# Weight halves in tiles of their own, and middle units of wide products run by row block, in a two-layer decoder trunk

## The chip, the cores and the metric

The kernel runs on one core of a Trainium2 chip. The metric is the device time of one execution in microseconds (us); the time of a version is the median of its runs. In the profile PE is the matrix engine (TensorE) and PEld its loading of the 128x128 operand, DVE is VectorE, ACT is ScalarE, POOL is GpSimd, and SP is the engine that issues the loads of the weights.

## The reference

Input are 256 tokens of width 2048, 256 memory tokens, and the f32 weights of two layers. A layer is a token mixer, a cross attention into the memory, and a squared-ReLU MLP, each one as x + norm(f(norm(x))).

```
for i in range(2):
    x = x + rms_norm(mixer_i(rms_norm(x)))          # i = 0: mLSTM, i = 1: gated DeltaNet
    x = x + rms_norm(cross_attention(rms_norm(x), mem))
    x = x + rms_norm(relu(rms_norm(x) @ w_up) ** 2 @ w_down)     # 2048 -> 8192 -> 2048
```

The mixer of layer 1, where most of what follows takes place, projects to q, k (16 heads of 128), v (32 heads of 128), z and the gates, runs q, k and v through a causal convolution of four taps and a silu, and solves a unit triangular system in chunks of 64 tokens:

```
q, k = l2_norm(silu(conv(q))), l2_norm(silu(conv(k)));  v = silu(conv(v))
g    = -exp(a_log) * softplus(a + dt_bias);  gam = cumsum(g)
A    = (k*beta) @ k.T * exp(strict_lower(gam_i - gam_j))
U, W = solve(I + A, v*beta), solve(I + A, k*beta*exp(gam))
```

## The kernel before

Some 500 MB of f32 weights are streamed from memory once, in **units** of 2048 columns per partition. `Weights` (L33 to L112) holds the list of all units in the order of use. A unit of a wide or a token product covers 4 row blocks of 128 by 512 columns, a **tall** unit (the products gq, gk and gv, and a few small ones) 16 row blocks by 128 columns. A unit is loaded in two halves of 512 KB by SP's queue (L74) into tiles `raw`, of which there are four. Each half is then split for the matrix engine: ACT copies it to the rounded type fp32r as `hi` (L88 CAST), and DVE takes `lo = raw - hi` (L89). Two tiles `hi` and two tiles `lo` of 8 KB per partition, each for a whole unit, turn around. `take` hands the oldest unit to a product and first begins those up to two ahead (L98).

Each product is the sum of hi*hi, hi*lo and lo*hi. The wide products (`prod_feat`, L286: k_m, q, k, o, up, and wide parts of the others) take one hi matmul of 512 columns (both parts of the activations) and one lo matmul of 256 (L314, L315), for 4 column blocks f times 4 row blocks j of a unit. The first unit of a product goes over all f for each j, every other one over all j for each f (L306 to L308). `prod_tall` (L325) takes a unit's 16 row blocks in order with three matmuls of 256 columns each (L333, L334 on hi, L335 on lo), so the second half's tiles come after 24 of its 48 matmuls. `prod_tok` (L356) has tokens as the stationary operand, three matmuls of 512 columns (L378, L379 on lo, L380); v, xq, xo, down, gz and g_out are of this kind.

The order of the instructions on each engine is not written out: a scheduler in the framework lists them from the program's order, the tiles' lifetimes and estimated times, and each engine then runs its list in order. When a tile is freed earlier or later on paper, instructions of all engines can change places.

In layer 1's mixer the q and k products run in four rounds (`prod_q`, `prod_k`, L949 and on). Beside them stand, per round, the convolutions of the blocks just made (`conv`: `pad` and three `cv` on DVE, one `cv` L868 and a silu L871 on ACT), `norms` (squares `l2sq` L962 on ACT, column sums `l` L966 on PE, an rsqrt L266 on ACT) and twice `pairs` (L969): `decays` multiplies masks into `gl` on POOL, sums them on PE (`gep`, L937) and takes 12 exps on ACT (`gdm`, L941); k times q and k times k on PE (`g`, L983, L984) are scaled on DVE and ACT (`gm`, L986 to L990) and multiplied with `gdm` on DVE (`at`, L994). Silu, exp and the rsqrt need tables that ACT loads when it goes from one to another (ACT_TABLE_LOAD). The gates run once before that: a softplus on DVE and ACT (`sp_e`, `sp_u`), then `g` (L913) and a matmul `suf` (L919). After the rounds come the v blocks (`prod_v`, with transposes `vp` L884) beside the solve, whose intermediate tensors go out and in by POOL's queue (`t_d`, `tn_d`, `ab`).

Of the kernel before, what the change touches and what calls it, by code (L numbers as in the profile page):

```python
# [8 lines left out]
F32R = mybir.dt.float32r  # L9
# [5 lines left out]
P = 128  # L15
# [19 lines left out]
class Weights:  # L35
# [18 lines left out]
    def begin(self, place=None):  # L54
# [8 lines left out]
        un = UN * UK // kb  # L63
        if place:
            hi, lo = zip(*(place(j) for j in range(kb)))
        else:
            ht = self.hi.tile([P, kb, un], F32R, tag="hi", name=f"hi{i}")
            lt = self.lo.tile([P, kb, un], F32R, tag="lo", name=f"lo{i}")
            hi, lo = ([t[:, j, :] for j in range(kb)] for t in (ht, lt))
        halves = []  # L70
        hb = kb // 2
        for k0 in range(0, kb, hb):
            raw = self.raw.tile([P, hb, un], F32, tag="raw", name=f"raw{i}_{k0}")
            nc.sync.dma_start(raw[:, :, :n], src[k0 * P : (k0 + hb) * P, :].rearrange("(kb p) n -> p kb n", p=P))  # L74

            def split(k0=k0, raw=raw):
                if kb == KB and n < P:
                    h_, l_ = ht[:, k0 : k0 + hb, 0:n], ht[:, k0 : k0 + hb, n : 2 * n]
                    a = nc.scalar.copy(h_, raw[:, :, :n])
                    return a, nc.vector.tensor_tensor(l_, raw[:, :, :n], h_, ALU.subtract)  # L80
                if place:
                    for j in range(hb):
                        h_ = hi[k0 + j][:, :n]
                        a = nc.scalar.copy(h_, raw[:, j, :n])
                        v = nc.vector.tensor_tensor(lo[k0 + j][:, :n], raw[:, j, :n], h_, ALU.subtract)
                    return a, v
                h_, l_ = ht[:, k0 : k0 + hb, :n], lt[:, k0 : k0 + hb, :n]
                a = nc.scalar.copy(h_, raw[:, :, :n])  # L88
                return a, nc.vector.tensor_tensor(l_, raw[:, :, :n], h_, ALU.subtract)  # L89
# [21 lines left out]
def trunk(ctx: ExitStack, tc, x, mem, norm_g, mem_norm_g, w_mem_kv, w_xq, w_xo, w_up, w_down,  # L111
# [5 lines left out]
    const = ctx.enter_context(tc.tile_pool(name="const", bufs=1))  # L117
    ws = Weights(tc, ctx, ahead=2, bufs=(4, 2, 2))
    acts = ctx.enter_context(tc.tile_pool(name="acts", bufs=1))
# [172 lines left out]
    def prod_feat(key, srcs, n_fb, evac, wide=True, before=None, fresh=False):  # L292
# [3 lines left out]
        for c0 in range(0, n_fb, 4):  # L296
            nf = min(4, n_fb - c0)
            accs, k = None, 0
            while k < nk:
# [6 lines left out]
                order = [(f, j) for f in range(nf) for j in range(kb)]  # L306
                if c0 == 0 and k == 0:
                    order = [(f, j) for j in range(kb) for f in range(nf)]  # L308
# [929 lines left out]
```

## Time and profile before

| what | value |
|---|---|
| time, median of 3 runs | 2954.86 us (2952.91 to 2958.61) |
| the profiled execution, its time / span | 2962.7 us / 2960.6 us |
| mean granted TensorE clock of it | 0.993 |
| PE busy | 2911.2 us (98%), 16595 matmuls |
| DVE / ACT / POOL busy | 1746.1 (59%) / 1443.7 (49%) / 137.1 us (5%) |
| bytes moved | 553.15 MB, mean 187 GB/s |

The page gives busy time by engine and the chain of work that ended last. Where one engine is busy nearly everywhere, the busy time by stretches of 100 us shows where it is not; the list of its waits by what released them, and the timeline of a stretch (one row per instruction, with the idle time before it and its releaser in brackets) then show why. Matmuls overlap, so the time from one start to the next, and not a row's duration, is what a matmul costs in a dense stretch.

### The profile page before, as it was taken

The numbers are of one execution on the slowest core, as the hardware profiler recorded it, in microseconds if no ns is written. First come the engines' busy times: TensorE is split into PE (matmuls) and PEld (weight loads), VectorE is DVE, ScalarE is ACT, GpSimd is POOL, SyncE is SP. The second block draws the span as 40 slices with busy tenths as digits, with TensorE's granted clock in tenths as the row PEclk, the third lists the DMA queues.
The fourth block names the chain that finished last, engine by engine and source line by source line (L and its number), as shares of the span: only waits on it lengthen the run. The fifth ranks groups of instructions, "written<-read, shape, count | busy, mean of one in ns | idle before, by whom it ended". The sixth has DMA issues, their size and how long they took to land.

```text
span 2960.6 us, 42191 instructions
## 1 busy us (share of the span) xinstructions
PE 2911.2 (98%) x16595; PEld 2504.0 (85%) x16595; DVE 1746.1 (59%) x2544; ACT 1443.7 (49%) x2213; POOL 137.1 (5%) x256
## 2 busy tenths in 40 slices
PE   8999999999999999999999999999999999999998
PEld 7888888988888888898889977877888888888887
DVE  5555657654645555677778844444567546455565
ACT  6444546544434444566664544444456444344343
POOL 0000000000000000013321011000000000000000
PEclk9999999999999999999999999999999999999999
DMA  7545565556655556556778755655445565555565
GB/s 232 178 157 158 192 199 167 168 186 194 189 189 187 193 186 196 180 150 167 204 204 226 240 200 182 212 182 172 162 149 185 186 197 185 191 191 189 188 190 170
DMA packets 373960, 553.15 MB, mean 187 GB/s; under 512 B 22769, under 2 KB 155378, under 8 KB 371458
## 3 DMA queue, kind: packets, MB, share of 16 engines
q1 hardware_dynamic: 363456, 507.12, 55.1%
q0 software_dynamic: 8736, 42.02, 4.1%
q8 instruction: 130, 2.13, 0.3%
q10 hardware_dynamic: 1570, 1.33, 0.1%
q14 instruction: 68, 0.56, 0.1%
HBM read 527.29 MB, written 23.10 MB: 186 GB/s over the span
## 4 chain that ended last, share of the span: by engine, by line
PE 92%; DMA 3%; DVE 3%; ACT 1%; issue 1%; DVEq 0%; ACTq 0%; SPq 0%
PE up L314 15%; PE up L315 8%; PE down L378 8%; PE down L380 8%; PE down L379 8%; DMA raw<-in_gdn_w_in 2%; PE gz L378 2%; PE gz L380 2%; PE gz L379 2%; PE g_out L378 2%; PE g_out L380 2%; PE g_out L379 2%; PE o L314 2%; PE gv L335 2%; PE gv L333 2%; PE gv L334 2%
## 5 line engine op out<-in xcount | busy, mean ns | idle before, releaser
L89 DVE TENSOR_TENSOR lo<-raw,hi 128x1024 fp32r<-128x1024 f32 x938 | 1121.4, 1224 | 901.3 <-ACT hi L88 900.4
L88 ACT CAST hi<-raw 128x1024 fp32r<-128x1024 f32 x938 | 947.6, 1046 | 972.2 <-PE down L380 310.8
L314 PE MATMUL up<-h,hi 128*128 128x512 f32 x1920 | 678.7, 399 | 0.0
L315 PE MATMUL up<-h,lo 128*128 128x256 f32 x1920 | 539.2, 281 | 0.0
L314 PEld LDWEIGHTS up<-h,hi 128*128 128x128 f32 x1920 | 360.8, 188 | 89.8
L379 PE MATMUL down<-lo,u 128*128 128x512 f32 x1024 | 398.4, 389 | 0.0
L378 PE MATMUL down<-hi,u 128*128 128x512 f32 x1024 | 398.4, 389 | 0.0
L380 PE MATMUL down<-hi,u 128*128 128x512 f32 x1024 | 398.3, 389 | 0.0
L315 PEld LDWEIGHTS up<-h,lo 128*128 128x128 f32 x1920 | 362.7, 189 | 0.2
L380 PEld LDWEIGHTS down<-hi,u 128*128 128x128 f32 x1024 | 192.2, 188 | 40.0
L378 PEld LDWEIGHTS down<-hi,u 128*128 128x128 f32 x1024 | 192.2, 188 | 40.0
L379 PEld LDWEIGHTS down<-lo,u 128*128 128x128 f32 x1024 | 192.2, 188 | 39.6
L333 PE MATMUL gv<-h,hi 128*128 128x256 f32 x512 | 148.6, 290 | 1.7 <-ACT hi L88 1.7
L335 PE MATMUL gv<-h,lo 128*128 128x256 f32 x512 | 147.9, 289 | 0.8 <-DVE lo L89 0.8
L334 PE MATMUL gv<-h,hi 128*128 128x256 f32 x512 | 147.6, 288 | 0.0
L378 PE MATMUL gz<-hi,h 128*128 128x512 f32 x256 | 103.7, 405 | 0.0
L380 PE MATMUL gz<-hi,h 128*128 128x512 f32 x256 | 103.0, 402 | 0.0
L333 PEld LDWEIGHTS gv<-h,hi 128*128 128x128 f32 x512 | 100.7, 197 | 2.7 <-ACT hi L88 2.3
L379 PE MATMUL gz<-lo,h 128*128 128x512 f32 x256 | 102.5, 400 | 0.0
L335 PEld LDWEIGHTS gv<-h,lo 128*128 128x128 f32 x512 | 100.6, 197 | 1.5 <-DVE lo L89 1.5
L334 PEld LDWEIGHTS gv<-h,hi 128*128 128x128 f32 x512 | 100.8, 197 | 0.3 <-issue 0.2
L378 PE MATMUL g_out<-hi,u 128*128 128x512 f32 x256 | 100.9, 394 | 0.0
(412 smaller groups left out, 4728.4 us busy)
## 6 DMA issues: line engine op xcount, KB each, us to landing
raw<-in_w_up SPq DMA_DIRECT2D x256, 512.0 KB, 3.9
raw<-in_w_down SPq DMA_DIRECT2D x256, 512.0 KB, 4.2
raw<-in_gdn_w_in SPq DMA_DIRECT2D x192, 512.0 KB, 4.9
raw<-in_mlstm_w_in SPq DMA_DIRECT2D x96, 512.0 KB, 4.0
raw<-in_gdn_w_out SPq DMA_DIRECT2D x64, 512.0 KB, 4.2
raw<-in_mlstm_w_out SPq DMA_DIRECT2D x32, 512.0 KB, 4.4
at_d<-at POOLq DMA_DIRECT2D x8, 1536.0 KB, 7.6
ab<-at_d POOLq DMA_DIRECT2D x8, 1536.0 KB, 8.6
```

Of the source, the lines that this page charges most:

```text
L88: a = nc.scalar.copy(h_, raw[:, :, :n])
L89: return a, nc.vector.tensor_tensor(l_, raw[:, :, :n], h_, ALU.subtract)
L314: PE.matmul(a[:fw], wh, srcs[kk][:, :], start=(kk == 0), stop=False, skip_group_check=True)
L315: PE.matmul(a[:fw, T:], wl, srcs[kk][:, 0:T], start=False, stop=(kk == nk - 1), skip_group_check=True)
L333: PE.matmul(a[:, 0:T], hi[k], srcs[k][:, 0:T], start=(k == 0), stop=False)
L334: PE.matmul(a[:, 0:T], hi[k], srcs[k][:, T:], start=False, stop=False)
L335: m = PE.matmul(a[:, 0:T], lo[k], srcs[k][:, 0:T], start=False, stop=(k == nk - 1))
L378: PE.matmul(accs[t], sh, hi[j], start=(kk == 0), stop=False)
L379: PE.matmul(accs[t], sh, lo[j], start=False, stop=False)
L380: PE.matmul(accs[t], sl, hi[j], start=False, stop=(kk == nk - 1))
```

## The change

The tiles `hi` and `lo` are taken per half unit: four of 4 KB each in place of two of 8 KB, so that the space is the same and each half is freed when its own last matmul is done. The cast L88 and the subtraction L89 (L93 and L94 in the new file, where lines behind them are 5 higher) write the same elements as before. In `prod_feat` the units that are neither first nor last of a product now also go over all f for each j, so that their first half is done after 16 of their 32 matmuls.

```diff
@@ -61,21 +61,26 @@
         k, n = src.shape
         kb, i = k // P, self.done
         un = UN * UK // kb
-        if place:
-            hi, lo = zip(*(place(j) for j in range(kb)))
-        else:
-            ht = self.hi.tile([P, kb, un], F32R, tag="hi", name=f"hi{i}")
-            lt = self.lo.tile([P, kb, un], F32R, tag="lo", name=f"lo{i}")
-            hi, lo = ([t[:, j, :] for j in range(kb)] for t in (ht, lt))
+        hi, lo = [], []
         halves = []
         hb = kb // 2
         for k0 in range(0, kb, hb):
             raw = self.raw.tile([P, hb, un], F32, tag="raw", name=f"raw{i}_{k0}")
             nc.sync.dma_start(raw[:, :, :n], src[k0 * P : (k0 + hb) * P, :].rearrange("(kb p) n -> p kb n", p=P))
-
-            def split(k0=k0, raw=raw):
+            if place:
+                ht = lt = None
+                ph, pl = zip(*(place(j) for j in range(k0, k0 + hb)))
+                hi += ph
+                lo += pl
+            else:
+                ht = self.hi.tile([P, hb, un], F32R, tag="hi", name=f"hi{i}_{k0}")
+                lt = self.lo.tile([P, hb, un], F32R, tag="lo", name=f"lo{i}_{k0}")
+                hi += [ht[:, j, :] for j in range(hb)]
+                lo += [lt[:, j, :] for j in range(hb)]
+
+            def split(k0=k0, raw=raw, ht=ht, lt=lt):
                 if kb == KB and n < P:
-                    h_, l_ = ht[:, k0 : k0 + hb, 0:n], ht[:, k0 : k0 + hb, n : 2 * n]
+                    h_, l_ = ht[:, :, 0:n], ht[:, :, n : 2 * n]
                     a = nc.scalar.copy(h_, raw[:, :, :n])
                     return a, nc.vector.tensor_tensor(l_, raw[:, :, :n], h_, ALU.subtract)
                 if place:
@@ -84,7 +89,7 @@
                         a = nc.scalar.copy(h_, raw[:, j, :n])
                         v = nc.vector.tensor_tensor(lo[k0 + j][:, :n], raw[:, j, :n], h_, ALU.subtract)
                     return a, v
-                h_, l_ = ht[:, k0 : k0 + hb, :n], lt[:, k0 : k0 + hb, :n]
+                h_, l_ = ht[:, :, :n], lt[:, :, :n]
                 a = nc.scalar.copy(h_, raw[:, :, :n])
                 return a, nc.vector.tensor_tensor(l_, raw[:, :, :n], h_, ALU.subtract)
 
@@ -115,7 +120,7 @@
     V, S, G, PE = nc.vector, nc.scalar, nc.gpsimd, nc.tensor
 
     const = ctx.enter_context(tc.tile_pool(name="const", bufs=1))
-    ws = Weights(tc, ctx, ahead=2, bufs=(4, 2, 2))
+    ws = Weights(tc, ctx, ahead=2, bufs=(4, 4, 4))
     acts = ctx.enter_context(tc.tile_pool(name="acts", bufs=1))
     tmp = ctx.enter_context(tc.tile_pool(name="tmp", bufs=2))
     small = ctx.enter_context(tc.tile_pool(name="small", bufs=2))
@@ -304,7 +309,7 @@
                 if accs is None:
                     accs = [acc(f"{key}{c0 + f}") for f in range(nf)]
                 order = [(f, j) for f in range(nf) for j in range(kb)]
-                if c0 == 0 and k == 0:
+                if (c0 == 0 and k == 0) or 0 < k < nk - kb:
                     order = [(f, j) for j in range(kb) for f in range(nf)]
                 w_ = wide and not (fresh and c0 == 0)
                 for f, j in order:
```

PE, DVE, POOL and SP execute the same instructions as before; ACT has 16 ACT_TABLE_LOAD more (67 in place of 51). Where they stand differs. The first place is PE in the second round of q and k, at the second pair group. `gk1` to `gk3` are column blocks of the k product with the units 224 to 226, `h8` its row block 8, the first of a unit's second half. Before:

```order
L983 MATMUL g0_11389<-gqk1_10431 128x512
L984 MATMUL g1_11390<-gqk1_10431 128x256
L937 MATMUL gep_11683<-gl00_11684,tri_gt_r_10420 128x512
L333 MATMUL gk1_11487<-h8_10283,hi224_11409 128x256
L334 MATMUL gk1_11487<-h8_10283,hi224_11409 128x256
L937 MATMUL gep_11683<-gl01_11686,tri_gt_r_10420 128x512
L333 MATMUL gk2_11555<-h0_10275,hi225_11477 128x256
L334 MATMUL gk2_11555<-h0_10275,hi225_11477 128x256
L937 MATMUL gep_11694<-gl10_11695,tri_gt_r_10420 128x512
```

and now, from the same matmul of `g` on:

```order
L988 MATMUL g0_11831<-gqk1_10851 128x512
L989 MATMUL g1_11832<-gqk1_10851 128x256
L339 MATMUL gk1_11933<-h8_10701,hi224_8_11857 128x256
L340 MATMUL gk1_11933<-h8_10701,lo224_8_11858 128x256
L338 MATMUL gk1_11933<-h9_10702,hi224_8_11857 128x256
```

followed by the rest of unit 224 without a break, to the first matmuls of units 225 and 226 and two of `gep`:

```order
L340 MATMUL gk1_11933<-h15_10708,lo224_8_11858 128x256
L338 MATMUL gk2_12003<-h0_10693,hi225_0_11923 128x256
L339 MATMUL gk2_12003<-h0_10693,hi225_0_11923 128x256
L338 MATMUL gk3_12073<-h0_10693,hi226_0_11993 128x256
L339 MATMUL gk3_12073<-h0_10693,hi226_0_11993 128x256
L942 MATMUL gep_12133<-gl00_12134,tri_gt_r_10840 128x512
L942 MATMUL gep_12133<-gl01_12136,tri_gt_r_10840 128x512
```

Unit 224's second half stood behind the matmuls of `gep` and was cut in two by them; now it follows at once, `gep` stands a unit later, and its last two pairs later still.

The second place is ACT at the same point, from the scaling of `gm` on. Before:

```order
L990 ACTIVATE gm_11376<-g0_11377,rk_11339 128x2x128
L88 CAST hi224_11409<-raw224_8_11413 128x1024
L868 ACTIVATE cv_11471<-pad_11468,cols_98 128x256
L88 CAST hi225_11477<-raw225_0_11479 128x1024
L88 CAST hi225_11477<-raw225_8_11481 128x1024
L990 ACTIVATE gm_11388<-g0_11389,rk_11339 128x2x128
L941 ACTIVATE gdm_11681<-gep_11683,lnb_11025 128x128 x2
L941 ACTIVATE gdm_11682<-gep_11683,lnb_11025 128x128 x2
L941 ACTIVATE gdm_11681<-gep_11694,lnb_11025 128x128 x2
L941 ACTIVATE gdm_11682<-gep_11694,lnb_11025 128x128 x2
L941 ACTIVATE gdm_11681<-gep_11705,sufb_11036 128x128 x2
L941 ACTIVATE gdm_11682<-gep_11705,sufb_11036 128x128 x2
```

and now:

```order
L995 ACTIVATE gm_11818<-g0_11819,rk_11781 128x2x128
L873 ACTIVATE cv_11915<-pad_11912,cols_98 128x256
L93 CAST hi225_0_11923<-raw225_0_11921 128x1024
L93 CAST hi225_8_11927<-raw225_8_11925 128x1024
L93 CAST hi226_0_11993<-raw226_0_11991 128x1024
L995 ACTIVATE gm_11830<-g0_11831,rk_11781 128x2x128
L93 CAST hi226_8_11997<-raw226_8_11995 128x1024
L946 ACTIVATE gdm_12131<-gep_12133,lnb_11459 128x128 x2
L946 ACTIVATE gdm_12132<-gep_12133,lnb_11459 128x128 x2
L93 CAST hi227_0_12063<-raw227_0_12061 128x1024
L876 ACT_TABLE_LOAD
L876 ACTIVATE gqk4_11472<-cv_11915 128x256
```

The cast of unit 224's second half has gone ahead of the first pair group's exps (out of these rows), four casts stand ahead of the second group's, and its 12 exps are no longer in one piece: four, then a silu with a table load before it, then the others in pieces between silus, each with a table load. This holds in all four rounds.

The third place is PE at the `suf` matmul of the gates, in the q product ahead of the rounds, before:

```order
L333 MATMUL gq2_11188<-h8_10283,hi221_11110 128x256
L334 MATMUL gq2_11188<-h8_10283,hi221_11110 128x256
L919 MATMUL suf_11034<-g_11027,tri_gt_95 128x32
L335 MATMUL gq2_11188<-h8_10283,lo221_11111 128x256
L333 MATMUL gq2_11188<-h9_10284,hi221_11110 128x256
```

and now:

```order
L339 MATMUL gq2_11628<-h2_10695,hi221_0_11548 128x256
L340 MATMUL gq2_11628<-h2_10695,lo221_0_11549 128x256
L924 MATMUL suf_11468<-g_11461,tri_gt_95 128x32
L338 MATMUL gq2_11628<-h3_10696,hi221_0_11548 128x256
L339 MATMUL gq2_11628<-h3_10696,hi221_0_11548 128x256
```

It stood at row block 8 of its unit, and now stands behind row block 2, 17 matmuls earlier.

## Rows read from the trace of the kernel before

**Rows 1.** The page: busy time by engine.

```profile
PE 2911.2 (98%) x16595; PEld 2504.0 (85%) x16595; DVE 1746.1 (59%) x2544; ACT 1443.7 (49%) x2213; POOL 137.1 (5%) x256
```

**Rows 2.** Windows of 100 us: busy us (instructions) by engine, PEclk, DMA share, GB/s.

```profile
700.00:800.00 100.00, 100.00 (x555) 86.28 (x555) 59.21 (x84) 46.89 (x69) 0.00 (x0) 1.00 0.59 186
1300.00:1400.00 100.00, 95.21 (x698) 88.91 (x698) 71.59 (x123) 64.53 (x111) 33.42 (x48) 0.97 0.58 158
```

**Rows 3.** What PE waited for: us in total, times, longest us.

```profile
PE gk L335 <- DVE lo L89: 5.3, 6, 1.2
PE l L966 <- ACT l2sq L962: 2.5, 3, 1.1
PE gv L333 <- ACT hi L88: 1.7, 2, 1.2
PE gk L333 <- ACT hi L88: 1.6, 3, 0.5
...
PE xo L379 <- DVE lo L89: 1.1, 2, 0.5
...
PE gv L335 <- DVE lo L89: 0.8, 1, 0.8
PE suf L919 <- DVE g L913: 0.6, 1, 0.6
```

**Rows 4.** Windows at the second pair groups of the three rounds and of the fourth.

```profile
1332.00:1342.00 10.00, 7.44 (x42) 5.29 (x41) 10.00 (x13) 8.75 (x20) 7.53 (x8) 1.00 0.28 93
1398.00:1408.00 10.00, 7.47 (x44) 5.42 (x43) 10.00 (x12) 8.85 (x19) 8.03 (x9) 1.00 0.34 112
...
1524.00:1532.00 8.00, 7.23 (x44) 5.66 (x43) 8.00 (x13) 7.72 (x19) 2.44 (x5) 1.00 0.42 139
```

**Rows 5.** Timeline of PE there, first round: start us, us, line, op [idle before <-releaser].

```profile
1333.77 0.39 PE L333 MATMUL gk<-h,hi 128*128 128x256 f32 x1 [0.54 <-ACT hi L88]
...
1336.38 0.39 PE L335 MATMUL gk<-h,lo 128*128 128x256 f32 x1 [0.56 <-DVE lo L89]
1336.60 0.28 PE L333 MATMUL gk<-h,hi 128*128 128x256 f32 x1
1336.72 0.28 PE L334 MATMUL gk<-h,hi 128*128 128x256 f32 x1
...
1341.34 0.39 PE L335 MATMUL gk<-h,lo 128*128 128x256 f32 x1 [1.21 <-DVE lo L89]
```

**Rows 6.** Timeline of ACT, same stretch, from the first group's exps on.

```profile
1325.79 1.91 ACT L941 ACTIVATE gdm<-gep,lnb 128x128 f32<-128x128 f32 x7
...
1331.34 1.03 ACT L88 CAST hi<-raw 128x1024 fp32r<-128x1024 f32 x1
...
1334.93 2.16 ACT L941 ACTIVATE gdm<-gep,lnb 128x128 f32<-128x128 f32 x8
1336.93 1.19 ACT L941 ACTIVATE gdm<-gep,sufb 128x128 f32<-128x128 f32 x4
1339.19 1.05 ACT L88 CAST hi<-raw 128x1024 fp32r<-128x1024 f32 x1 [1.06 <-PE gk L334]
```

**Rows 7.** Timeline of DVE, same stretch.

```profile
1331.52 1.83 DVE L994 TENSOR_TENSOR at<-gm,gdm 128x768 f32<-128x768 f32 x2
...
1336.25 3.50 DVE L994 TENSOR_TENSOR at<-gm,gdm 128x768 f32<-128x768 f32 x2
```

**Rows 8.** Groups by line and form, PE: line, op, names, count | busy us, mean ns | idle.

```profile
L314 PE MATMUL up<-h,hi 128*128 128x512 f32 x1920 | 678.7, 399 | 0.0
...
L314 PE MATMUL o<-h,hi 128*128 128x512 f32 x256 | 89.0, 392 | 0.0
```

**Rows 9.** Groups of ACT, 1236 to 1560 us: table loads for silu.

```profile
L871 ACT ACT_TABLE_LOAD x10 | 12.8, 1283 | 0.2
```

**Rows 10.** Timeline of ACT at the solve's end, the cast that PE waits for.

```profile
1688.06 1.04 ACT L88 CAST hi<-raw 128x1024 fp32r<-128x1024 f32 x1 [6.45 <-PE gv L335]
```

**Rows 11.** Window behind the solve's end, at the half clock.

```profile
1691.00:1694.40 3.40, 3.40 (x18) 3.40 (x17) 2.28 (x5) 1.43 (x3) 0.00 (x0) 0.50 0.74 187
```

## The prediction, made before the change was run

> **What bounds the kernel now.** I read the page's first part first: PE is busy for 2911.2 of 2960.6 us [rows 1], so all that any edit can win without shortening matmuls is about 49 us. The windows of 100 us say where those lie. In the MLP's stretches PE is busy for 100.00 of 100.00 us, where layer 1's q and k are made for 95.21 [rows 2]. Then I read the list of PE's waits, and kept those that end with a weight half, since the change is about these: lo for gk 5.3 us in 6 waits, hi for gk 1.6 us in 3, hi and lo for gv 1.7 and 0.8, lo for xo 1.1 [rows 3]. That is 10.5 us in all, and no wide product is on the list. The edit's evident aim, weights a half unit earlier, can so win in few places.
>
> The main place is the second pair group of each round. In the window of 10 us there PE is busy for 7.44 us in the first round and 7.47 in the second (the third is like it), and in the fourth, beside gv, for 7.23 of 8.00 [rows 4]: 2.56 + 2.53 + 2.53 + 0.77 = 8.4 us idle. The timeline shows three stops for a weight half, of 0.54, 0.56 and 1.21 us [rows 5], and the timeline of ACT why: after the exps of the first group, begun at 1325.79, the cast of the next half begins at 1331.34; then come 2.16 + 1.19 us of exps, and the next cast begins at 1339.19 [rows 6]. On DVE two `at` products take 3.50 us in that place against 1.83 for two a little earlier [rows 7], because DVE shares this stretch with POOL's masks (an inference: POOL is busy for 7.53 of these 10 us [rows 4]). So PE waits for casts that stand behind exps in ACT's order, and for lo behind `at` in DVE's.
>
> **The change part by part.** *Wide products, units run by row block first.* Costed at nothing. No wait for a weight stands there (`up` and o have an idle of 0.0 [rows 8]), and ACT and DVE with their casts and subtractions are busy for only 47 and 59 us of 100 [rows 2], so the earlier release is hidden by a PE that is never late. The order itself could cost or win through PE's pace: the hi matmul of `up` takes 399 ns on average, that of o 392 [rows 8], with the same shapes, and both have units of either order, since the first unit of a product is by row block already. If all 1920 of `up` went over to o's pace, 1920 x 7 ns = 13.4 us would be won; if the 512 of q, k and o went over to that of `up`, 512 x 7 ns = 3.6 us lost. I take 0, since in the trace the pace goes with the product and not with the order; the ends stay for the range.
>
> The Trainium skill (TensorE: Matmul & The Clock Gate, "Why this matters for your kernels") speaks against row blocks first: it wants all K tiles of one output tile in a row before going on. By its reasons the order matters where PE waits between them; by this trace PE does not wait there at all, so the sum by the rule is the same 0 as long as the units stay dense.
>
> *Rounds of q and k.* The order shows the cast of a unit's second half ahead of the first group's exps, four casts ahead of the second group's, and unit 224 run without a break. So the waits for hi of 0.54 us and for lo of 0.56 and 1.21 us [rows 5] lose their cause. Each stop also costs a slower restart: the first matmul after it takes 0.39 us against 0.28 in a dense stretch [rows 5], 0.1 us, four stops to a round. A round now loses 2.54 + 0.4 = 2.9 us. What stays: the lo of units 225 and later still stands among `gm` and `at` on DVE, which the change leaves slow (3.50 us [rows 7]); I leave 0.9 us, between nothing and the 0.56 + 1.21 = 1.8 us that the two waits for lo keep if they only go to a later unit. That gives 2.0 us a round, 6.0 for three, with bounds of 8.7 won (all gone) and, were a round's wait to grow by one more pair of `at`, 3 x (3.5 - 2.0) = 4.5 lost. For the fourth, beside gv, 0.77 + 0.1: I take 0.9, bounds 0 and 1.1.
>
> *The 16 table loads.* Each takes 1283 ns [rows 9], so 20.5 us more on ACT, 5.1 in each of four rounds of about 64 us. ACT is busy for 64.53 of 100 us there [rows 2], so of 64 us about 23 are free, and 5.1 fit. They are costed at nothing: what hides them is this idle time, and a cast that may come late by the slack between its unit and PE, which is up to a unit, 48 matmuls x 0.12 us = 5.8 us (from one start to the next they take 0.12 us in a dense stretch [rows 5]). If that cover is gone the price is up to 5.1 us a round, the second rival.
>
> *The gates.* `suf` waits for `g` on DVE now (0.6 us [rows 3]) and moves 17 matmuls earlier, 17 x 0.12 = 2.0 us, while what makes `g` (softplus on DVE and ACT) is not shortened. If `g` comes as now, PE stands for 2.0 us longer; if the matmul that feeds the chain and two casts ahead of its table load (1.05 us each [rows 6]) also delay it, 4.1. At best the chain moves up with it and the cost is 0. I take 2.0, as the nearest row, bounds 0 and 4.1. Queued behind `suf` on PE are the other matmuls of gq, nothing that another engine is short of.
>
> *End of the solve.* PE waits there once for hi of gv, 1.2 us of the 1.7, and 0.8 for lo [rows 3], and behind it 3.40 us run at the granted clock 0.50 [rows 11], that is at 1.2 GHz, after a PE that stood still; half of these 3.4 us, 1.7, is the loss. The cast waited 6.45 us for a matmul's release of a tile [rows 10], and a half tile is released up to 24 matmuls, 2.9 us, earlier. So the 2.0 go and half of the clock's loss: -2.9, bounds 0 (the raw half is not there sooner, since POOL's transfers fill the DMA engines) and -3.7.
>
> *xo.* 1.1 us [rows 3] in two layers. Its casts can start when half a unit is free. I take -1.1, bounds 0 and -1.1 (an end with more in it has no row).
>
> *The rest.* SP's queue gives out the same loads with the same four `raw` tiles. The waits of `l` for `l2sq`, 2.5 us [rows 3], stand behind squares that do not move; 0. Clock windows elsewhere may come and go, 1.7 us each as at the solve: ±3 for the range.
>
> Sum: 0 - 6.0 - 0.9 + 0 + 2.0 - 2.9 - 1.1 = -8.9 us. The profiled execution took 2962.7 us and would take 2953.8. It is 7.8 us above the median of the runs, 2954.86; the terms are stalls that every run should have, so I take the sum off the median: **2946.0 us**.
>
> **The rivals.** *The wait only moves.* PE, no longer stopped at the second pair group, comes 2.9 us sooner to `l`, which waits for `l2sq` already (0.8 us on average [rows 3]), or to weights that the loads do not bring sooner. Then the rounds' 6.9 us come back, and what is left is 2.0 - 2.9 - 1.1 = -2.0: 2952.9 us, no difference that can be measured (0.2%, 5.9 us, is about what a measurement of this kernel tells from none). For it: l2sq is made on ACT behind the same exps and table loads. Against it: of the three waits for `l`, the longest is 1.1 us, while a round's idle time at the pair group is 2.5. That the halves are not cast sooner, because `raw` and not `hi` is what is missing, ends in the same place: without the solve's term and xo's, and with half of the rounds', -3.4 + 2.0 = -1.4, 2953.4 us.
>
> *The split exps reach PE.* ACT runs its list in order. In place of one block of exps it now goes exp, silu, exp, silu, with a table load each; a silu waits for `cv` on DVE, and casts stand behind it. If the casts between them come a load and a silu's wait too late, PE stops once for each. Price: 5.1 us a round in four, 20.5, against the -8.9 of the sum: 2954.9 - 8.9 + 20.5 = 2966.5 us, slower. It decides from the point at which the loads and waits in a unit's 5.8 us, with 2 casts (2.1 us), a `cv` and a silu (0.9), exceed what is left, 2.8 us: two table loads (2.6) and one exp make that full. For it speaks that some units get two loads; against it that other units have the whole 2.8 us free and casts can run ahead by a unit.
>
> The Trainium skill (ScalarE: Activation LUTs, "Table sets: the hidden batching unit") gives the rule that this breaks: all activations of one set together, then those of the next. It puts a switch at 2.66 us including a drain, by which 16 would cost 42.6 us of ACT; the trace shows 1283 ns a load and the next activation directly behind it, so the price above goes by the trace.
>
> *PE's pace changes.* `up` goes over to o's pace: -8.9 - 13.4 = -22.3, 2932.6 us. For it: the two paces exist with the same shapes. Against it: units by row block first occur at the start of `up` and go no faster.
>
> **How the numbers follow.** The forecast has 0.50, and with it go 2937 to 2953 (all bounds for the better; rounds halved and the gates at their worse end). The wait that moves and the missing `raw` together 0.28, the exps that reach PE 0.16, the pace 0.06. Faster by over 0.2%: 0.50 + 0.06 = 0.56; within: 0.28; slower: 0.16. The range reaches to the pace's case at 2932 and on the other side to 2962, three quarters of the exps' price; outside is the worst of the exps' case and a pace that goes with all terms for the better.
>
> **What would show it right or wrong.** In the list of PE's waits gk for lo and hi falls from 6.9 us to under 3, gv's 2.5 to under 1, xo's 1.1 to about 0, and `suf` grows from 0.6 to about 2.6. In the windows at the pair groups PE is busy for over 9 us of 10. ACT's table loads in the rounds rise by 16, with ACT near 70 of 100 us. `up` keeps 399 ns. Wrong would be: waits for l or for a DMA grown by what gk's lost, waits for hi behind a table load, or wide matmuls of another mean length.

## The result and the profile after

| | median | runs | lowest to highest |
|---|---|---|---|
| before | 2953.56 us | 20 | 2949.28 to 2958.61 |
| changed | 2960.39 us | 20 | 2956.22 to 2964.23 |

The ratio is 1.0023 with a 95% interval of 1.0016 to 1.0030: the change costs about 7 us. Forecast were 2946.0 us and, with 0.56, a gain; the time lies inside the range of 2932 to 2962, on the side that had 0.16.

The page hardly shows it. Busy time by engine of the changed kernel, in answer to [rows 1]:

```profile
PE 2911.4 (98%) x16595; PEld 2501.9 (85%) x16595; DVE 1777.1 (60%) x2544; ACT 1496.4 (51%) x2229; POOL 140.7 (5%) x256
```

PE has the same work; ACT has 52.7 us more, of which 20.5 are the 16 table loads and some 30 come from casts that overlap each other less (a cast takes 1047 ns on average, 1046 before). The two profiled executions took 2962.7 and 2961.98 us, so their traces alone would have shown no loss; the one of before was longer than all of its other runs (2949 to 2959), the one of after is within its own. What they lost the time to differs, and the list of PE's waits shows it. In answer to [rows 3]:

```profile
PE g L989 <- ACT gdm L946: 12.7, 4, 3.4
PE ltp L215 <- DVE xk L495: 10.1, 9, 1.8
...
PE gk L340 <- DVE lo L94: 3.6, 3, 1.3
PE l L971 <- ACT l2sq L967: 2.6, 3, 1.1
...
PE gv L340 <- DVE lo L94: 0.2, 1, 0.2
PE suf L924 <- DVE g L918: 0.2, 1, 0.2
```

Most of the waits that the prediction counted did go: gk for hi is no longer there (1.6), gk for lo is 3.6 for 5.3, gv's two are 0.2 for 2.5, xo's have gone, `vp`'s 2.7 and `gep`'s 1.0 too (both from the list of before), and `suf` is 0.2 for 0.6. In their place stands one that was not on the list before: the matmul `g` waits for the exps `gdm`, four times, 12.7 us in all, the longest 3.4. The whole list comes to 40.1 us before and 39.4 now: what the half tiles won, `g` took back.

The windows in answer to [rows 2] show the MLP's stretch dense as before (PE busy for all of 700 to 800 us) and the rounds as bad as before, with ACT at 68.68 for 64.53:

```profile
1300.00:1400.00 100.00, 95.07 (x705) 89.49 (x704) 70.91 (x118) 68.68 (x116) 32.95 (x46) 0.97 0.56 152
```

In answer to [rows 8] the mean of `up`'s hi matmul is the same, and that of o has gone from 392 to 399 ns:

```profile
L319 PE MATMUL up<-h,hi 128*128 128x512 f32 x1920 | 678.7, 399 | 0.0
...
L319 PE MATMUL o<-h,hi 128*128 128x512 f32 x256 | 90.7, 399 | 0.0
```

That is 256 x 7 ns = 1.8 us lost, by which o as a whole also takes longer from start to start. It is the pace that the prediction gave a rival, but the other product and the other way.

**Where `g` stands still.** The timeline of PE in the first round, second pair group, of the changed kernel (start us, us, line, op, and in brackets the idle time before it and its releaser):

```profile
1337.10 0.38 PE L340 MATMUL gk<-h,lo 128*128 128x256 f32 x1 [1.18 <-DVE lo L94]
...
1345.82 1.02 PE L988 MATMUL g<-gqk 128*128 128x512 f32 x2
...
1351.26 0.70 PE L989 MATMUL g<-gqk 128*128 128x256 f32 x2 [3.11 <-ACT gdm L946]
```

The wait for lo of 1.18 us at 1337.10 is what is left of the three stops of [rows 5]. The new one is 3.11 us, at 1351.26; with it PE is busy for 6.89 of the 10 us from 1342, where the first round's window of [rows 4] had 7.44. ACT in the same stretch:

```profile
1332.62 1.14 ACT L946 ACTIVATE gdm<-gep,lnb 128x128 f32<-128x128 f32 x4
1336.40 1.05 ACT L93 CAST hi<-raw 128x1024 fp32r<-128x1024 f32 x1 [2.64 <-DMA raw<-in_gdn_w_in]
1337.46 1.28 ACT L876 ACT_TABLE_LOAD   x1
1338.76 0.42 ACT L876 ACTIVATE gqk<-cv 128x256 f32<-128x256 f32 x1
...
1339.59 1.28 ACT L946 ACT_TABLE_LOAD   x1
1340.89 0.37 ACT L946 ACTIVATE gdm<-gep,lnb 128x128 f32<-128x128 f32 x1
...
1345.54 1.05 ACT L93 CAST hi<-raw 128x1024 fp32r<-128x1024 f32 x1 [3.88 <-PE gk L340]
1346.49 0.36 ACT L946 ACTIVATE gdm<-gep,lnb 128x128 f32<-128x128 f32 x1
1346.87 1.28 ACT L876 ACT_TABLE_LOAD   x1
1348.16 0.72 ACT L876 ACTIVATE gqk<-cv 128x256 f32<-128x256 f32 x2
1348.89 1.28 ACT L946 ACT_TABLE_LOAD   x1
1350.18 0.37 ACT L946 ACTIVATE gdm<-gep,lnb 128x128 f32<-128x128 f32 x1
...
1350.85 0.36 ACT L946 ACTIVATE gdm<-gep,lnb 128x128 f32<-128x128 f32 x1
```

The first four exps of this group are done by 1333.8. Then ACT comes to a cast, waits 2.64 us for its raw half, casts, does a table load and a silu, a table load and one exp (1340.89), and comes to the next cast, which starts at 1345.54 after 3.88 us of idleness. The three exps behind it that read the same PSUM bank follow at 1346.49, 1350.18 and 1350.85, with two table loads and two silus between. `gep` and the tiles of `g` take turns in three PSUM banks (tag `ps`, three buffers), so the second `g` tile can't be written until the last of these exps has read its bank: 1350.85 + 0.36 = 1351.21, and PE starts at 1351.26. Two things so lie between PE and its bank: the 3.88 us of idleness, and behind it the split, of which the two table loads alone are 2.56 us. By these rows the wait of 3.11 us would be 0.55 us without these two table loads, and nothing without the idleness (an estimate, all else left as it is).

The row puts the 3.88 us down to a matmul of gk, but gk's matmuls end without a break all the time there; the load of the half says more. The DMA issues of `raw` between 1336.5 and 1339 us (count, time on the queue, and us to landing):

```profile
L69 SPq DMA_DIRECT2D raw<-in_gdn_w_in x2: 367/367/367, 1337.1 to 1339.0; - x2
...
DMA to landing us min/median/max: 8.3/8.5/8.7
```

The first was issued at 1337.1 and landed 8.3 us later, at 1345.4, 0.1 us before the cast begins. In the same microseconds POOL's queue stores the first pair group's `at`, 1.5 MB (issued at 1335.9, landed 7.7 us later), and the blocks `a_d`. The page of before has for both (KB, median us to landing):

```profile
raw<-in_gdn_w_in SPq DMA_DIRECT2D x192, 512.0 KB, 4.9
...
at_d<-at POOLq DMA_DIRECT2D x8, 1536.0 KB, 7.6
```

In the kernel before, loads of 8 us stand in this place too, but ACT had done all 12 exps by 1338.1 [rows 6] before it came to the casts.

So the order of [rows 6] was bad for PE in one way, and protected it in another. It let exps go ahead of casts. The changed kernel lets casts go ahead of exps, and one of these casts waits for a load.

**The granted clock.** The time of a run goes with its mean granted TensorE clock: among the 21 runs of before beside the first experiments, 0.997 and 0.998 go with 2948.6 to 2950.9 us, 0.994 with 2952.8 to 2958.5. A clock c on average over T means that (1 - c) x T was lost where PE sets the pace (at half clock for 2(1 - c)T). The means of all runs are 2952.9 us with 0.9956 before and 2960.1 us with 0.9942 for the changed kernel: lost to the clock are 12.9 and 17.2 us, 4.3 of the 7.2 us of difference (with the 27 runs of before beside the second experiments, mean 0.9961, it would be 5.6). The rest, 2940.0 and 2943.0, differs by 3 us. The list accounts for part of it: without `ltp` and `cps` it was 17.6 us before (with the rows left out of [rows 3]) and is 19.5 now, `ltp` for `xk` has gone from 12.0 to 10.1, and o has lost 1.8; the slower restarts are not in the list. By these means over half of the loss came by the clock. In the trace it is low right behind the new stops, in the windows of 3.4 us after the four waits of `g` (PEclk is the third number from the right):

```profile
1352.90:1356.30 3.40, 3.40 (x13) 2.70 (x12) 3.31 (x8) 3.37 (x5) 0.06 (x1) 0.50 0.00 0
1417.80:1421.20 3.40, 3.40 (x9) 2.19 (x9) 2.98 (x6) 3.37 (x7) 0.10 (x1) 0.51 0.05 13
1486.00:1489.40 3.40, 3.40 (x8) 2.36 (x9) 2.81 (x7) 3.38 (x7) 0.10 (x1) 0.50 0.07 17
1550.90:1554.30 3.40, 3.40 (x10) 2.08 (x10) 3.14 (x8) 3.27 (x6) 0.10 (x1) 0.51 0.18 71
```

All four are at 1.2 GHz, the lower level. They are not the only ones: between 1230 and 1700 us this trace has 10.2 us more at that level (behind waits of `l` of 0.4 and 1.1 us), 23.8 in all, and the trace of before has 23.8 there too (behind stops of `ltp`, `l`, `vp` and gv of 0.5 to 2.3 us). The execution profiled of before was its slowest; so that the changed kernel loses 4 us more by the clock rests on the means of the runs, and that the waits of `g` are the reason is argued from their place.

### The profile page after: what moved, and what is told of

Read it like the earlier page. It is cut to its first block, busy times and chain, and to the rows that moved or that the text cites. A ratio compares the mean times of both kernels' runs of the same rounds, so it can differ in the third digit from the quotient of the medians.

```text
span 2960.3 us, 42654 instructions
## 1 busy us (share of the span) xinstructions
PE 2911.4 (98%) x16595; PEld 2501.9 (85%) x16595; DVE 1777.1 (60%) x2544; ACT 1496.4 (51%) x2229; POOL 140.7 (5%) x256
## 3 DMA queue, kind: packets, MB, share of 16 engines
q0 software_dynamic: 8736, 42.02, 4.2%
## 4 chain that ended last, share of the span: by engine, by line
PE 49%; DVE 2%; ACT 1%; DMA 1%; issue 1%; POOL 0%; DVEq 0%; ACTq 0%; POOLq 0%; SPq 0%
PE up L319 8%; PE down L384 4%; PE down L383 4%; PE down L385 4%; PE up L320 4%; PE gz L383 2%; PE gz L384 2%; PE g_out L383 2%; PE g_out L384 2%; PE gz L385 2%; PE g_out L385 2%; PE gv L340 1%; PE gv L338 1%; PE gv L339 1%; DMA raw<-in_gdn_w_in 1%; PE wp L1150 1%
## 5 line engine op out<-in xcount | busy, mean ns | idle before, releaser
L94 DVE TENSOR_TENSOR lo<-raw,hi 128x1024 fp32r<-128x1024 f32 x938 | 1143.5, 1223 | 875.9 <-ACT hi L93 856.4
L93 ACT CAST hi<-raw 128x1024 fp32r<-128x1024 f32 x938 | 977.8, 1047 | 935.3 <-PE down L385 333.2
L383 PEld LDWEIGHTS down<-hi,u 128*128 128x128 f32 x1024 | 192.2, 188 | 40.1
L385 PEld LDWEIGHTS down<-hi,u 128*128 128x128 f32 x1024 | 192.2, 188 | 40.1
L875 DVE SCALAR_TENSOR_TENSOR cv<-pad,cols,cv 128x256 f32<-128x256 f32 x192 | 98.1, 520 | 21.4 <-issue 11.6
L383 PE MATMUL g_out<-hi,u 128*128 128x512 f32 x256 | 101.1, 395 | 0.0
L384 PE MATMUL g_out<-lo,u 128*128 128x512 f32 x256 | 100.9, 394 | 0.0
L385 PE MATMUL g_out<-hi,u 128*128 128x512 f32 x256 | 100.0, 392 | 0.0
```

The costliest lines, as they stand in the source:

```text
L383: PE.matmul(accs[t], sh, hi[j], start=(kk == 0), stop=False)
L384: PE.matmul(accs[t], sh, lo[j], start=False, stop=False)
L385: PE.matmul(accs[t], sl, hi[j], start=False, stop=(kk == nk - 1))
L875: V.scalar_tensor_tensor(c, pad[:, j : j + T], w[j], c, ALU.mult, ALU.add)
```

## Theories

- **A, banks:** `g` waits because exps hold the PSUM banks; take the banks apart or the exps together and 13 us come back.
- **B, row blocks:** the new order of middle units costs in the wide products.
- **C, loads:** the 16 table loads, and the split by itself, are the price.
- **D, a late load:** A's banks are held because a cast stands ahead of the exps on ACT and waits for a raw half, which the store of `at` holds up.

## The experiments

All ratios are to the kernel before, run on the same chip in the same hour. Times of different experiments are partly from different hours, in which the kernel before had medians from 2953.1 to 2954.8 us.

**The parts of the change.** First the tiles alone, with the order of wide units as before:

```diff
-                if (c0 == 0 and k == 0) or 0 < k < nk - kb:
+                if c0 == 0 and k == 0:
```

> The changed kernel with the old order in wide products: only the half-unit tiles are left of the change. Theory A (the loss lies in layer 1's q and k rounds: there a matmul g waits 12.7 us in four waits for the exps that read the PSUM banks of gep, because half tiles let casts in and split the exps): ACT and PE stand in the same order there as in the changed kernel, so about 2960 us, ratio to before 1.002, with the four waits of g for gdm at 12 to 13 us. Theory B (the row-block order of middle units costs in the wide products): about 2953, ratio 1.000. If the row-block order wins something that the rounds hide: slower than 2960.

Measured: 2964.93 us, ratio 1.0043 (1.0030 to 1.0056).

```profile
PE g L989 <- ACT gdm L946: 11.8, 4, 3.2
```

The waits of `g` for `gdm` are there, so the tiles alone bring the loss, as A said; it is even larger than with both parts, mostly by the clock (on average 22.0 us lost to it, against 17.2). B falls. Then the row blocks alone, on the kernel before:

```diff
-                if c0 == 0 and k == 0:
+                if (c0 == 0 and k == 0) or 0 < k < nk - kb:
```

> The kernel before with only the row-block order of middle units, tiles of a whole unit as before. Theory A: the rounds stand as before (no split exps), no wait of g for gdm, ratio 1.000 +- 0.001, about 2953. Theory B: about 2960, ratio 1.002. The mean of up's hi matmul stays at 399 ns by A.

Measured: 2954.43 us, ratio 1.0004 (0.9994 to 1.0013); `up` has 399 ns, o 392. The waits are those of before (gk 5.3 us for lo and 1.6 for hi, xo 1.0 for lo). The row-block order alone is worth nothing, as the prediction had it. With half tiles it is not quite so: 2964.93 against 2960.39 without and with it, and again below.

**Banks.** The second tile of each `g` pair from the products' five banks:

```diff
-                    p0, p1 = psum("g0"), psum("g1")
+                    p0, p1 = psum("g0"), acc("g1")
```

> The changed kernel with the second of the two PSUM tiles of each g pair taken from the five banks of the products instead of the three that it shares with gep. The exps of the second pair group then stand nearly in one block on ACT, but there are 67 table loads as in the changed kernel. Theory A (banks): the four waits of g for gdm, 12.7 us with restarts of some 1 us each, are gone, about 2960 - 13 = 2947, ratio 0.998. Theory C (the 16 more table loads are the price, by what they take from ACT): still about 2960, ratio 1.002, with the waits gone to hi or lo of gk or gq.

Measured: 2957.32 us, ratio 1.0016 (1.0007 to 1.0024). The expectation by A missed: the wait has not gone, it has moved to the other `g` tile and grown.

```profile
PE g L988 <- ACT gdm L946: 19.4, 4, 5.7
```

What ACT did in that place (first round):

```profile
1344.18 1.05 ACT L93 CAST hi<-raw 128x1024 fp32r<-128x1024 f32 x1 [4.24 <-DMA raw<-in_gdn_w_in]
...
1350.37 0.37 ACT L946 ACTIVATE gdm<-gep,lnb 128x128 f32<-128x128 f32 x1
```

The scheduler has put the exps later, behind two more casts, and the first of these waits 4.24 us for a load; exps begin at 1350.37. The bank is only where the lateness shows. That is what made D out of A. It is no clean test of banks, since the order on ACT changed with it.

**The pair group ahead of the k product.**

```diff
                     pairs(c * 2 - 2)
+                    pairs(c * 2 - 1)
                 prod_k(c)
                 if c == 0:
                     lnb, gh, gl, sufb = gates()
-                else:
-                    pairs(c * 2 - 1)
             prod_v(0)
             norms(3)
             pairs(6)
+            pairs(7)
             prod_v(1)
-            pairs(7)
```

> The changed kernel with the second pair group of a round written ahead of the k product instead of behind it: its exps then stand right behind those of the first group in two blocks, with 51 table loads as before, and gep's six matmuls within 14 others. Theory A: no wait of g for gdm beyond 0.5 us each, since nothing stands between the matmuls of gep and their exps; about 2946 to 2950, ratio 0.997 to 0.999. Theory C gives the same, as the loads are gone. If the casts behind 24 exps come too late, the waits for hi and lo of gk come back (2.9 us a round as before): about 2955.

Measured: 2942.05 us, ratio 0.9964 (0.9951 to 0.9976). Faster than both kernels, and 4 us below what was expected. In its trace nothing of `gdm` holds PE:

```profile
PE gq L340 <- DVE lo L94: 3.4, 3, 1.9
PE gv L340 <- DVE lo L94: 2.1, 3, 1.4
PE g L989 <- DVE gm L993: 2.0, 3, 0.7
```

Its mean clock is 0.9978, a loss of 6.5 us to the clock where before has 12.9. It does not tell C from D, since the loads are gone and the exps stand ahead of the casts. The same edit on the kernel before (lines as above):

> The kernel before, whole-unit tiles, with the second pair group written ahead of the k product as in the run that did so with half tiles (2942). If that run's time comes from the half tiles once the exps are out of the way: this one at about 2950, ratio 0.999. If it comes from the place of the pair group alone: about 2942, ratio 0.996.

Measured: 2954.24 us, ratio 1.0007 (0.9998 to 1.0016).

```profile
PE g L984 <- DVE gm L988: 4.8, 3, 1.6
PE gq L335 <- DVE lo L89: 3.4, 2, 1.9
PE gv L335 <- DVE lo L89: 3.4, 3, 2.0
```

With whole tiles the gain is not there: `g` waits longer for the scaling on DVE, and gq and gv for their lo halves (these three 11.6 us, and gv 2.2 for hi). So half tiles and row blocks are worth 12 us in this order, more than was forecast for them. And the half tiles without row blocks in that order (the first diff on top of this one):

> Half-unit tiles and the second pair group ahead of the k product, without the row-block order of middle units. If the row-block order is worth nothing also where the rounds are clean: 2942 as with it, ratio 0.996. If it takes part in the gain: 2945 to 2950.

Measured: 2948.91 us, ratio 0.9985 (0.9976 to 0.9994), 7 us above the run with row blocks. The waits in the rounds are alike; the one that differs most is the feed of a stage, where `ltp` waits for `xk`, 10.1 us with a longest of 1.8 in the run with row blocks:

```profile
PE ltp L215 <- DVE xk L495: 13.0, 9, 2.9
```

By the means the difference is nearly all clock: 12.1 us lost to it against 6.5, and 2936.3 against 2935.8 of rest. Why the row blocks save clock here is not settled: outside the rounds the scheduler also put instructions of DVE and ACT in other places. That these stops are longer without row blocks is what the traces show.

**Loads alone.** The kernel before with 16 table loads added, by an exp of one column behind two silus in each k product:

```diff
             S.activation(dst, c, AF.Silu)
-
+            if ch in TWICE:
+                S.activation(warm2[:, :], c[:, 0:1], AF.Exp)
+
+        TWICE = {16, 17, 20, 21, 24, 25, 28, 29}
         vts, padded = {}, []
+        warm2 = small.tile([P, 1], F32, bufs=1, name="warm2")
```

> The kernel before with 16 table loads added: in the k product of each round two silus are each followed by an exp of one column, which forces a load to exp and one back to silu. Exps of the pair groups stay in their two blocks. Theory C (the loads are the price): 4 x 1.28 us a round on ACT, slower by 4 to 10 us, ratio 1.002 or more. Theories A and D: the loads fit into ACT's idle time and hold no PSUM bank, ratio 1.000 +- 0.001.

Measured: 2959.01 us, ratio 1.0023 (1.0014 to 1.0032). C's number; the expectation by A and D missed. The wait of gq is new, that of gk has fallen from 5.3:

```profile
PE gq L335 <- DVE lo L89: 5.0, 2, 2.9
PE gk L335 <- DVE lo L89: 4.0, 5, 1.2
```

and ACT, first round:

```profile
1348.22 1.05 ACT L88 CAST hi<-raw 128x1024 fp32r<-128x1024 f32 x1 [3.05 <-DMA raw<-in_gdn_w_in]
...
1351.11 1.28 ACT L871 ACT_TABLE_LOAD   x1
...
1352.84 1.28 ACT L873 ACT_TABLE_LOAD   x1
...
1354.36 1.28 ACT L871 ACT_TABLE_LOAD   x1
```

The place suggests why. A cast has just waited 3.05 us for its raw half (1348.22), and behind it and one more cast stand three table loads, 3.8 us, ahead of the next casts (1356.37), whose lo PE then waits for. The prediction costed the table loads at nothing because ACT is idle for a third of the time on average; but from 1300 to 1500 us of the kernel before that idle time ends for 22 us with a raw half and for 30 us with `cv` on DVE, and what stands behind such a wait is late already. That this is all of the 5.5 us is not shown: the list of PE's waits is only 1 us longer than before (the waits of `l`, 2.5 us, have gone, for one), and the scheduler also moved casts, squares and a scaling in the rounds, so the table loads are not all that differs. Whether they are what costs in the changed kernel, the next runs tell.

**The store of `at` made small.** In the changed kernel and in the kernel before:

```diff
-                nc.gpsimd.dma_start(at_d[grp], at)
+                nc.gpsimd.dma_start(at_d[grp][:, 0:2], at[:, 0:2])
...
-                nc.gpsimd.dma_start(ab, at_d[grp])
+                for i_ in range(0, 6, 2):
+                    nc.gpsimd.dma_start(ab[:, i_ : i_ + 2], at_d[grp][:, 0:2])
```

> The changed kernel with a third of what `at` stores: only its first two of six blocks go out (0.5 MB instead of 1.5 MB per pair group) and these are read back three times, so the mixer's result is left wrong; every engine's order in the rounds is that of the changed kernel, 67 table loads too. Theory D (a cast that stands ahead of the remaining exps on ACT waits for its raw half, whose load takes 8 to 9 us because the 1.5 MB store fills the DMA engines; the exps behind it hold the PSUM banks, and g waits): the loads land some 2.4 us sooner, the cast's idle time on ACT falls from 3.9 us to about 1.5, the four waits of g for gdm from 12.7 us to 3 to 6, time about 2952, ratio 1.000. Theory C (the split and its table loads by themselves): g still waits 12 us, ratio 1.002.

Measured: 2934.17 us, ratio 0.9935 (0.9922 to 0.9949), 18 us below what D gave; the wait of `g` fell further than to the 3 to 6 us expected. PE, DVE, ACT and SP run the same order as in the changed kernel. In the first round the half that took 8.3 us lands in 4.8, and its cast waits 0.61 us in place of 3.88; the row now names the load:

```profile
PE g L989 <- ACT gdm L946: 0.6, 2, 0.4
...
1343.41 1.05 ACT L93 CAST hi<-raw 128x1024 fp32r<-128x1024 f32 x1 [0.61 <-DMA raw<-in_gdn_w_in]
```

> The kernel before with a third of what `at` stores, as in the run that did so with the changed kernel (2934); again two of six blocks go out and are read back three times, so the mixer's result is left wrong. It is the base for that run. Theory D (the loss of the change needs the late load): with the load on time the half tiles win what the prediction gave them, some 9 us, so this one is at 2941 to 2946, slower than 2934. If the half tiles lose or win nothing even then: about 2934. Waits of gk for lo stay (5 us), as they come from exps and `at` ahead of the cast and not from the load.

Measured: 2945.01 us, ratio 0.9974 (0.9964 to 0.9984). Its waits for weights are about those of before: gk 4.1 us for lo and 1.6 for hi, gv 2.0 for hi.

With the load on time `g` waits 0.6 us in place of 12.7, although the exps are split and the 67 table loads are all there; C would have left the wait. And against its own base the change now wins: 2934.17 - 2945.01 = -10.8 us, near what was forecast (-8.9). The nearness is in part luck: PE's waits are 8.2 us shorter, but 5.5 us of the gain is clock (7.0 us lost to it against 12.5), which the forecast had at next to nothing, and some of it goes back to a slower pace, o's 1.8 among it. The missing megabyte is worth 8 us to the kernel before and 26 to the changed one.

**The store in two.** Nothing left out, no engine's order in the rounds changed:

```diff
                     for v2 in range(2):
                         ...
+                    nc.gpsimd.dma_start(at_d[grp][:, :, kh * 2 : kh * 2 + 2], at[:, :, kh * 2 : kh * 2 + 2])
-                nc.gpsimd.dma_start(at_d[grp], at)
```

> The changed kernel with the store of `at` in two of 0.75 MB, each behind the products of its half of the heads, and nothing else: the order of all engines in the rounds, the split exps and the 67 table loads are those of the changed kernel. Theory D (the load held up by the store keeps the cast, the exps behind it and so g waiting): the first half goes out some 4 us earlier, the loads behind it land 2 to 4 us sooner, the waits of g for gdm fall from 12.7 to under 5 us, time 2944 to 2950, ratio 0.997 to 0.999. Theory C (split exps and their loads by themselves): g waits 12 us, ratio 1.002.

Measured: 2944.82 us, ratio 0.9966 (0.9954 to 0.9979).

```profile
PE g L989 <- ACT gdm L946: 6.1, 4, 2.6
```

The half now lands in 6.4 us. The cast that was at 1345.54 starts at 1340.89, with 1.93 us of waiting for its load in place of 3.88 (the other 2.70 us are a lead that the kernel has from earlier places), and the last exp of the bank is done at 1346.56:

```profile
1340.89 1.05 ACT L93 CAST hi<-raw 128x1024 fp32r<-128x1024 f32 x1 [1.93 <-DMA raw<-in_gdn_w_in]
...
1346.20 0.36 ACT L946 ACTIVATE gdm<-gep,lnb 128x128 f32<-128x128 f32 x1
```

The wait of `g` is halved, 6.1 us, a little more than expected; the time is in the middle of what D gave. One line, which moves a transfer and no instruction of PE, DVE, ACT or SP, turns the change from 7 us lost to 10 us won. Of the 15.6 us between the two, PE's waits are 8.7 (`g` 6.6 of them) and the clock 6.9 (10.3 us lost to it in place of 17.2). With one store, two, and a third of it the cast waits 3.88, 1.93 and 0.61 us and `g` 12.7, 6.1 and 0.6 us in all, with the split and the 67 table loads in place each time. That settles D: the split exps cost because a late load stands in front of them. What is not settled is why two stores hold the loads up less: the first goes out earlier, each is half as large, and POOL's queue moves the same 42.02 MB in more packets (10912 in place of 8736). Nor was the store in two run on the kernel before, so how much of the 10 us is the change's own is open.

**Both together**, the pair group first and the store in two:

> The changed kernel with the second pair group ahead of the k product, and the store of `at` in two of 0.75 MB, each behind the products of its half of the heads. Theory D: the load behind the first store is held up for half as long, waits of gq and gv for lo (3.4 and 2.1 us in the run with one store) fall to under 3 together, 2938 to 2941, ratio 0.995. If two transfers of half the size hold up the loads as long as one, or pieces of 1 KB are slower: 2942 to 2946.

Measured: 2936.03 us, ratio 0.9943 (0.9929 to 0.9956), the best of the kernels that compute all, 17 us faster than before and 24 than the changed kernel. gq's and gv's waits for lo are 2.8 us where they were 5.5, as expected, and the time is 2 us below what was expected. It lost 7.0 us to the clock, about as with one store (6.5), so the 6 us gained are not clock; but the scheduler moved `at` on DVE and a cast on ACT with it, and o is back at 392 ns, so they are not the store's alone.

**Three hi, five raw.** The changed kernel with `bufs=(5, 3, 4)`:

> The changed kernel with five raw, three hi and four lo half tiles (the same space). By the order the exps of the second group stand in one block again, 51 table loads, and one cast only stands ahead of them. Theory D: no wait of g for gdm, more loads under way, waits for lo of gk at the second pair group as before: 2948 to 2953, ratio 0.998 to 1.000. If half tiles cost by themselves in the wide products: over 2956.

Measured: 2953.20 us, ratio 1.0001 (0.9992 to 1.0009), at the end of what was expected. With three hi tiles the 12 exps stand in a block as before, and gk's waits (5.2 us for lo, 1.6 for hi) and the time are those of before. No wait of `g`. That does not show a fifth raw tile to be worth nothing: PE's waits in its trace are 31 us in all (40 before), while `up` and `down` take 6.5 us longer from start to start, and their weight loads, which hardly waited for lo before (0.2 us), now do so (here `up`; idle us of PEld in the last columns):

```profile
L320 PEld LDWEIGHTS up<-h,lo 128*128 128x128 f32 x1920 | 362.6, 189 | 8.6 <-DVE lo L94 7.2
```

## Why the prediction was wrong, step by step

- *What bounds the kernel, and where weights are waited for:* right. The weight waits stood where it said, and 6.7 of the 10.5 us it counted went.
- *Wide products by row block, nothing:* right for the part alone (1.0004). `up` kept its pace. o lost 1.8 us to the slower pace, within the bounds given. In the runs it follows neither part of the change: o has 399 ns in the changed kernel, with the pair group first (with row blocks and without), with the store in two and with the small store, and 392 with each part alone, with the other banks and with pair group and store together. So "the pace goes with the product and not with the order" does not hold, and what sets it is open.
- *Rounds, -6.0:* half. Hi of gk went; lo keeps one stop of 1.2 to 1.3 us a round. 3.3 us in waits. The reading put all three stops down to exps and `at`; [rows 6] shows that the cast behind the longest one waited 1.06 us more for a matmul of gk to release its tile. In a kernel whose loads come in time the whole change won 10.8 us (-8.9 forecast), of which PE's waits are 8.2.
- *The 16 table loads and the split exps around them, nothing:* **this is the step that failed.** What it put at nothing cost 12.7 us in waits of `g` for `gdm`. The prediction looked at how much time ACT had, 23 of 64 us, and not at what ACT waited for in that time. It read the order of ACT, saw casts go ahead of the exps, and counted that as a gain for PE's weights alone. It did not ask what was queued behind those casts: exps, which hold the banks that `g` needs next. Nor did it ask whether the data of a cast moved ahead would be there: the page's DMA part has a transfer of 1.5 MB per pair group on another queue, and the cast waited 3.88 us for its load in the first round.
- *The gates, +2.0:* wrong in sign; `suf` waits 0.2 us in place of 0.6, so the chain moved up with it, the end of the range that was given as the best.
- *The solve's end, -2.9, and xo, -1.1:* right. gv 0.2 us in place of 2.5, no xo on the list, and the window of half clock behind the solve is not in the trace of after.
- *The clock, 0 with ±3:* the size was wrong, 4.3 us more lost on average. In the trace the clock is at its lower level behind each of the four stops of 3 us.
- *The second rival* had the right sign and the right engine, and 0.16. Its price, 20.5 us, was made of table loads behind which casts stand; what happened was the reverse, exps behind a cast that waits for its load, with table loads between these exps. None of the signs that the prediction named for being wrong was a wait of `g`. The 12.7 us of waits, 4.3 us of clock and 1.8 us of o's pace ate the 8.9 us of the forecast and 7 more.

## What to carry to other kernels

When an edit lets a copy go earlier in an engine's list, ask what it now stands in front of, and whether its input will be there: an engine that runs its list in order passes a late load on to everything behind it, and work that holds PSUM banks passes it on to PE. Idle time of an engine is room for more work only where the engine is not waiting for the thing that the new work stands behind. A large store that meets the loads may be worth more than the buffers: here a store cut in two, at the same bytes, gave 15 us to the changed kernel.

## What the runs showed of the hardware

- Loads of 512 KB on SP's queue that were issued during a store of 1.5 MB from POOL's queue took between 8 and 10 us to land in the changed kernel, where the page of before has a median of 4.9 us; behind the first store of a round cut to 0.5 MB they took 4.5 to 5.4 us.
- A table load takes 1.28 us, and the next activation starts 0.02 us behind it (changed kernel, 1337.46 + 1.28, next row at 1338.76). The Trainium skill (ScalarE: Activation LUTs, "What ACT_TABLE_LOAD costs") has a drain of 1380 ns with it, 2.66 us for a switch; these rows show none.
- The spread of a kernel's times, 10 us among 21 runs of before, goes with the granted clock: from 0.994 to 0.998, some 12 us by (1 - c) x T. The run with the pair group first, whose stops in the rounds are 1.9 us at most, has a mean of 0.998.
- The same matmul of o took 392 ns on average in some kernels and 399 in others, though its own instructions were the same: 399 with the pair group first, 392 with the store in two on top of that.
